# A larger part of an output projection among the steps of a state recurrence

## The chip, the cores and the metric

The kernel runs on one core of one Trainium2 chip. The metric is the device time of one execution in microseconds (us). Before the change three runs gave 1123.08, 1124.1 and 1125.31 us; their median, 1124.1 us, is the time before.

## The reference, cut to what matters

One layer of a hybrid trunk runs over 640 tokens (128 of context, 512 latent ones) of width 1024:

```python
h = rms_norm(x, norm1_g) * (1 + scale1) + shift1
proj = h @ w_in
y_a = rwkv_mixer(shifted proj, s0, ...)   # 8 heads of 64, two directions
y_b = fourier_mixer(...)                  # "FNet", 256 channels
y_c = pool_mixer(...)                     # pooling, 256 channels
mixed = concatenate([y_a, y_b, y_c])      # 1024 channels
x = x + gate1 * (mixed @ w_out)
h = rms_norm(x, norm2_g) * (1 + scale2) + shift2
x = x + gate2 * (relu(h @ w_ff1) ** 2 @ w_ff2)
```

The shift, scale and gate terms, called the modulation here, are `silu(cond) @ w_ada + b_ada`, with one `cond` for the context tokens and one for the latent ones.

## The kernel before, in words

**Tiles.** Channels lie on the 128 partitions and tokens on the free axis, so 1024 channels are 8 blocks (`KB`) of 128 x 640. A product in full precision is made of three fast matmuls: every weight and activation tile is split in a high part (ScalarE copy) and a low part (a subtraction on VectorE or GpSimd), and `gemm_steps` (L333) issues high x high, high x low and low x high for each half of 320 tokens, so 6 matmuls for one 128 x 128 weight block (a "kb" below).

**Order.** `build` (L274) writes the instructions out in one fixed order for each engine. Up to the last state group, `run_groups` (L1367) chooses that order with a clock of its own (`Clock`, L164): fixed and per-element costs of each engine's operations, and for a DMA a fixed part and a rate. The state recurrence (`prep`, `group`) consists of 24 groups: four head pairs j = 0 to 3, three token ranges, two directions. When all six groups of a pair have ended, `post` (L1337) normalises its output y and stores it to the DRAM tile `ycd[j]`.

Beside the groups stand queues of other work. `gemms` holds large products, of which one matmul or two at a time are put where a group would leave TensorE waiting for over 50 ns of that clock (`gemm_step`), or where their share falls under the floor `MR` (0.15, but zero in the second of four stages of six groups); where no product is ready and the gap is over 150 ns, a matmul on a mask (`lmask`, 128 x 512), whose result nobody reads, is issued instead. `side`, `aux` and `slow` hold work that is stepped between the groups.

When the remaining input projection (`in_rest`) has ended, `second` (L1563) puts into `gemms` the modulation for shift2, scale2 and the two gates (`ada_steps`, L390: 64 weight tiles of 256 KB, loaded `AH` = 3 ahead), and into `slow` one task, `more`, that runs `fnet` (L566), then `pool_mix` (L629), then `prepare_out` (L1525), one after the other. `prepare_out` loads `ycd[4]` to `ycd[7]` (FNet and pooling) and splits them to `mh` and `ml`, transposes x into `x1`, and then appends `out_half` (L1508) to `gemms`: the product of the lower four kb of `w_out` for all 8 output blocks b, each added to `x1` under its gate by three VectorE operations (`gated`, L1501). What the queues still hold when the last group has ended is written out behind it, round robin.

**Behind the groups** (L1595 to L1620) the kernel loads `ycd[0]` to `ycd[3]`, splits them, and makes for each block b the upper four kb of `w_out` (24 matmuls), adds them to `x1` with `gated`, splits the scaled result into `h2h` (ScalarE) and `h2l` (VectorE), squares it (ScalarE) and sums the squares (`ssq`, GpSimd). The first block of `w_ff1` follows (8 kb, 48 matmuls, `ahead`), then the statistics of the norm, then the rest of the feed-forward part, in which TensorE sets the pace to the end.

Every operation passes through one wrapper (`Timed`, L251), so the profile shows line L251 for all; the tile names tell them apart: `raw`, `whi`, `wlo` are a weight block and its parts, `wa` modulation weights, `xr`, `W`, `EB`, `bda`, `P`, `X`, `oopa` belong to a state group, `pb` is a PSUM bank (8 in all).

Of the kernel before, what the change touches and what calls it, by code (L numbers as in the profile page):

```python
# [55 lines left out]
AH = 3  # L56
# [46 lines left out]
RS = 1024.0  # L103
AHEAD = 4
# [59 lines left out]
class Clock:  # L164
# [4 lines left out]
    DMA = 2200.0  # L169
    BW = 180.0  # L170
    BWL = 100.0
# [102 lines left out]
def build(nc, tc, T):  # L274
# [115 lines left out]
    def ada_steps(ks, slots, nk, ahead, queue=None):  # L390
# [14 lines left out]
        for n, (k, h, k2) in enumerate(todo):  # L405
# [13 lines left out]
            yield  # L419
# [577 lines left out]
    aux, preps, side, slow, gemms = queues = [[] for _ in range(5)]  # L997
# [14 lines left out]
    tail = [None]  # L1012
# [324 lines left out]
    def post(c):  # L1337
# [27 lines left out]
        S.dma_start(ycd[j][:], y[:])  # L1365

    def run_groups(todo):  # L1367
# [20 lines left out]
        def gemm_step():  # L1388
            t = clock.free["P"]
            step(gemms)  # L1390
            spent[0] += clock.free["P"] - t

        while todo or active or prepared or preps:
# [15 lines left out]
            if then and tail[0].state == "end" and not aux:  # L1409
                then.pop(0)()  # L1410

            urgent = [q for q in (side, aux) if q and not any(x[0] in ctx for x in todo) and todo]
            for n in range(q_.NB):
# [10 lines left out]
                for q in ((aux, slow, side) if slow and turn % q_.SLT == 0 else (aux, side, slow)):  # L1424
# [15 lines left out]
            if gemms and (late_g and used[0] < q_.URG * used[1] or spent[0] < q_.MR * (now - t0)):  # L1440
# [82 lines left out]
    es2 = ExitStack()  # L1523

    def prepare_out():  # L1525

        rx = es2.enter_context(tc.tile_pool(name="rx", bufs=1, side="right"))
        ra = mcs.enter_context(tc.tile_pool(name="ra", bufs=1, side="right"))
        x1 = late["x1"] = rx.tile([P, KB, NT], F32, name="x1")
        mh = late["mh"] = ra.tile([P, 4, NT], F32R, name="mh")  # L1530
        ml = late["ml"] = ra.tile([P, 4, NT], F32R, name="ml")
        loads = [ycd[4 + kb][:] for kb in range(4)] + [x for x in xin]
        place = []

        def load():
            if loads:
                src = loads.pop(0)
                place.append(ra.tile([P, D], F32, tag="xq", name="xq", bufs=2))
                S.dma_start(place[-1][:, 0:src.shape[1]], src)

        load()
        load()
        for kb in range(4):
            yc = place.pop(0)[:, 0:NT]
            yield yc
            S.copy(mh[:, kb, :], yc)
            yield
            (G if EPL else V).tensor_tensor(ml[:, kb, :], yc, mh[:, kb, :].bitcast(F32), op=ALU.subtract)
            yield
            load()  # L1550
        for t in range(5):
            x = place.pop(0)
# [461 lines left out]
```

## Time and profile before

| | before |
|---|---|
| median of 3 runs | 1124.1 us (1123.08 to 1125.31) |
| the profiled execution | 1125.89 us |
| its span, first to last instruction | 1124.1 us |
| TensorE busy | 1075.0 us (96%) |
| VectorE busy | 649.2 us (58%) |
| ScalarE busy | 566.1 us (50%) |
| GpSimd busy | 375.5 us (33%) |
| mean granted TensorE clock | 0.983 of full |

The page lists TensorE as PE (matmuls) and PEld (weight loads, which overlap them), VectorE as DVE, ScalarE as ACT, GpSimd as POOL, and the queue that issues most DMAs as SP. Ends of pipelined matmuls are modelled, so a start-to-start distance tells more of their cost than a duration. Idle time of an engine matters only where something later waits for it.

### The profile page before, as it was taken

What the parts mean: (1) busy time and instruction counts of PE and PEld (TensorE: products, weight loads), DVE (VectorE), ACT (ScalarE), POOL (GpSimd) and SP (SyncE); (2) the same over time, 40 slices, a digit from 0 to 9 for tenths busy, and PEclk for the clock granted to TensorE, in tenths of its full rate; (3) what the DMA queues carried; (4) which work ended last, traced back from release to release, by engine and by line L of the source; (5) the groups of instructions that cost most, each with busy time, mean ns of one, the idle gap of its engine ahead of it and who ended that gap; (6) DMA issues with size and microseconds to landing.
All of it is one profiled execution on the core that took longest, in us unless ns stands there. A gap on an engine that the chain in (4) does not pass through costs nothing.

```text
span 1124.1 us, 23713 instructions
## 1 busy us (share of the span) xinstructions
PE 1075.0 (96%) x9364; PEld 927.2 (82%) x9372; DVE 649.2 (58%) x1462; ACT 566.1 (50%) x1417; POOL 375.5 (33%) x445
## 2 busy tenths in 40 slices
PE   5999999999999998998999899999999999999996
PEld 3688878888786665655688799999999999999996
DVE  5256665457756564757754674773782287139513
ACT  5224576556467454664674265762572176126511
POOL 4224422123322231473500173354343235343120
PEclk9999999999999999999999999999999999999999
DMA  9523311211214345542321321225133123211312
GB/s 316 196 43 92 98 38 43 64 52 47 81 58 140 97 150 143 149 129 86 87 80 43 102 85 57 76 84 160 58 94 94 57 76 104 85 52 53 103 38 94
DMA packets 117712, 104.11 MB, mean 93 GB/s; under 512 B 8925, under 2 KB 95970, under 8 KB 117602
## 3 DMA queue, kind: packets, MB, share of 16 engines
q1 hardware_dynamic: 101618, 81.22, 23.5%
q10 hardware_dynamic: 15552, 21.05, 6.3%
q8 instruction: 74, 1.21, 0.5%
q0 software_dynamic: 432, 0.33, 0.2%
q14 instruction: 36, 0.29, 0.1%
HBM read 90.52 MB, written 9.76 MB: 89 GB/s over the span
## 4 chain that ended last, share of the span: by engine, by line
PE 74%; issue 8%; DVE 8%; ACT 3%; POOL 3%; DMA 2%; ACTq 1%; SPq 0%; POOLq 0%; DVEq 0%
PE pb L251 74%; DMA raw<-w_ff 1%; DVE t L251 1%; ACT pb L251 1%; DVE EB L251 1%; ACTq L251 1%; DVE bda L251 1%; POOL st L251 1%; POOL wlo L251 1%; DMA wa<-w_ada 1%; DVE P L251 1%; DVE BK L251 0%; DMA x<-x_sample 0%; ACT fh L251 0%; DVE op L251 0%
## 5 line engine op out<-in xcount | busy, mean ns | idle before, releaser
L251 POOL TENSOR_TENSOR wlo<-raw,whi 128x512 fp32r<-128x512 f32 x77 | 105.3, 1370 | 144.5 <-ACT whi L251 143.2
L251 PE MATMUL pb<-op,fhi 128*128 128x320 f32 x672 | 147.9, 308 | 0.0
L251 ACT CAST whi<-raw 128x512 fp32r<-128x512 f32 x113 | 70.0, 621 | 146.5 <-PE pb L251 105.1
L251 DVE SCALAR_TENSOR_TENSOR x<-pb,mod,x 128x128 f32<-128x128 f32 (+1 forms) x144 | 55.1, 434 | 147.6 <-PE pb L251 147.5
L251 PE MATMUL pb<-fh,whi 128*128 128x320 f32 (+2 forms) x408 | 123.1, 309 | 1.1 <-ACT fh L251 1.1
L251 PE MATMUL pb<-fl,whi 128*128 128x320 f32 (+2 forms) x408 | 123.1, 309 | 0.2
L251 PEld LDWEIGHTS pb<-op,fhi 128*128 128x128 f32 x672 | 112.4, 188 | 0.0
L251 PE MATMUL pb<-op,flo 128*128 128x320 f32 x336 | 103.5, 308 | 0.0
L251 PE MATMUL pb<-hhi,whi 128*128 128x320 f32 (+1 forms) x304 | 100.1, 334 | 0.0
L251 PE MATMUL pb<-hlo,whi 128*128 128x320 f32 (+1 forms) x304 | 99.5, 332 | 0.0
L251 PE MATMUL pb<-fh,wlo 128*128 128x320 f32 (+2 forms) x408 | 94.9, 308 | 0.3 <-POOL wlo L251 0.3
L251 POOL TENSOR_TENSOR flo<-rw,fhi 128x512 fp32r<-128x512 f32 x36 | 55.3, 1548 | 103.6 <-ACT fhi L251 84.5
L251 POOL TENSOR_TENSOR t<-t,k 128x256 f32<-128x256 f32 (+1 forms) x24 | 16.3, 679 | 205.9 <-DVE t L251 195.2
L251 PE MATMUL pb<-hhi,wlo 128*128 128x320 f32 (+1 forms) x304 | 79.4, 331 | 0.0
L251 PEld LDWEIGHTS pb<-fh,whi 128*128 128x128 f32 x408 | 76.5, 188 | 1.6 <-ACT fh L251 1.6
L251 PEld LDWEIGHTS pb<-fl,whi 128*128 128x128 f32 x408 | 76.6, 188 | 0.7 <-DVE fl L251 0.7
L251 ACT COPY W<-pb 128x256 f32<-128x256 f32 (+3 forms) x144 | 54.5, 399 | 41.2 <-DVE W L251 29.1
L251 PEld LDWEIGHTS <-bda 128*128 128x128 f16 x880 | 43.0, 99 | 37.7 <-issue 14.0
L251 PEld LDWEIGHTS pb<-fh,wlo 128*128 128x128 f32 x408 | 68.7, 188 | 0.5 <-POOL wlo L251 0.5
L251 POOL TENSOR_TENSOR st<-st,halfm 128x1 f32<-128x1 f32 (+2 forms) x19 | 24.2, 1275 | 125.6 <-DVE st L251 125.6
L251 PEld LDWEIGHTS pb<-hlo,whi 128*128 128x128 f32 x304 | 58.8, 194 | 7.6 <-issue 5.1
L251 ACT CAST bda<-pb 64x256 f16<-64x256 f32 (+1 forms) x192 | 63.8, 332 | 1.7
(285 smaller groups left out, 2713.2 us busy)
## 6 DMA issues: line engine op xcount, KB each, us to landing
raw<-w_ff SPq DMA_DIRECT2D x80, 256.0 KB, 2.8
wa<-w_ada SPq DMA_DIRECT2D x64, 256.0 KB, 3.1
rw<-w_ff SPq DMA_DIRECT2D x24, 512.0 KB, 3.6
wa<-w_ada SPq DMA_DIRECT2D x16, 512.0 KB, 8.9
raw<-w_in SPq DMA_DIRECT2D x30, 256.0 KB, 3.0
raw<-w_out SPq DMA_DIRECT2D x16, 256.0 KB, 2.9
ukd<-shq ACTq DMA_DIRECT2D x9, 320.0 KB, 2.5
ds<-dft_s ACTq DMA_DIRECT2D x8, 257.0 KB, 2.7
```

The lines of the kernel that those rows point to most:

```text
L251: return fn(out, *a, **k)
```

## The change

Of the output projection only the kb of the last head pair (j = 3) stays behind the groups. `out_half` becomes `out_part`, which runs twice: over the lower four kb once the modulation has ended, and over the three kb of the pairs 0 to 2 once pair 2 is done. The last pair's y is split from SBUF (`y3`) and no longer goes through DRAM; its weights are loaded and split by `out_last` once the second part has ended. `fnet` and `pool_mix` are two tasks in two queues (`slow`, `slow2`), and `prepare_out` starts when both have ended. From the start of the modulation on, products get at least the share `GR` = 0.3 of the planner's TensorE time while one is ready. Behind the groups the 6 matmuls of the last pair's kb for block b alternate with the first block of `w_ff1` for kb b - 1. The planner's DMA model is faster. The diff, cut:

```diff
-AH = 3
+AH = 5
...
+GR = 0.3
...
-    DMA = 2200.0
+    DMA = 1900.0
     BW = 180.0
-    BWL = 100.0
+    BWL = 260.0
...
             V.tensor_copy(asb[:], ps[:])
-            yield
+            yield asb[:]
...
-    aux, preps, side, slow, gemms = queues = [[] for _ in range(5)]
+    aux, preps, side, slow, slow2, gemms = queues = [[] for _ in range(6)]
...
-    tail = [None]
+    tail = [None, SimpleNamespace(state="end")]
...
-        S.dma_start(ycd[j][:], y[:])
+        if j < NJ - 1:
+            S.dma_start(ycd[j][:], y[:])
+        else:
+            mh, ml = late["y3"]
+            S.copy(mh[:, 0, :], y[:])
+            V.tensor_tensor(ml[:, 0, :], y[:], mh[:, 0, :].bitcast(F32), op=ALU.subtract)
...
-            step(gemms)
+            n = next((n for n, x in enumerate(gemms) if hasattr(x.state, "tensor") and x.state.tensor.name.startswith("asb")), None)
+            if n is None:
+                n = next((n for n, x in enumerate(gemms) if x.ready <= t + 200.0), 0)
+            if not gemms[n].step():
+                gemms.pop(n)
...
-            if then and tail[0].state == "end" and not aux:
+            if then and all(t.state == "end" for t in tail) and not aux:
...
-                for q in ((aux, slow, side) if slow and turn % q_.SLT == 0 else (aux, side, slow)):
+                for q in (aux, side, slow, slow2) if turn % 2 else (aux, side, slow2, slow):
...
+            if "ada" in late and "since" not in late:
+                late["since"] = now, spent[0]
+            since = late.get("since")
+            short = since and spent[0] - since[1] < GR * (now - since[0]) and min([x.ready for x in gemms], default=SLT) <= now + q_.GE
+            if gemms and (late_g and used[0] < q_.URG * used[1] or spent[0] < q_.MR * (now - t0) or short):
...
-            if gap > q_.GAP and gemms and gemms[0].ready <= now + q_.GE:
+            if gap > q_.GAP and gemms and min(x.ready for x in gemms) <= now + q_.GE:
...
-    def out_half():
-
-        w = wsplit(w_out, 0, 1, G if EWO else V)
+    def out_part(r0, nk, m):
+
+        def load(b):
+            if b < KB:
+                r = wp.tile([P, 4, P], F32, tag="raw", name="raw", bufs=RB)
+                dma(r[:, 0:nk], w_out[:, r0:r0 + nk, b * P:(b + 1) * P])
+                hi, lo = [wp.tile([P, 4, P], F32R, tag=n, name=n) for n in ("whi", "wlo")]
+                S.copy(hi[:, 0:nk], r[:, 0:nk])
+                (G if EWO else V).tensor_tensor(lo[:, 0:nk], r[:, 0:nk], hi[:, 0:nk].bitcast(F32), op=ALU.subtract)
+                return hi, lo
+
+        w = load(0)
         for b in range(KB):
             pss = [pm(), pm()]
-            for k4 in range(4):
-                if k4 == 1 and b + 1 < KB:
-                    w2 = wsplit(w_out, (b + 1) * P, 1, G if EWO else V)
-                for _ in gemm_steps(pss, w, (late["mh"], late["ml"]), k4, k4 == 0, k4 == 3):
+            for k4 in range(nk):
+                if k4 == 1:
+                    w2 = load(b + 1)
+                for _ in gemm_steps(pss, w, m, k4, k4 == 0, k4 == nk - 1):
                     yield w[1]
                 yield w[1]
             w = w2
             for h in range(2):
                 gated(late["x1"][:, b, :], pss[h], h, 2, b, late["x1"][:, b, :])
 
...
+    def out_last():
+
+        late["w"] = []
+        for n in range(2):
+            r = wp.tile([P, 4, P], F32, tag="raw", name="raw", bufs=RB)
+            dma(r[:], w_out[:, 3, 512 * n:512 * (n + 1)].rearrange("p (b c) -> p b c", c=P))
+            yield r[:]
+            late["w"].append(wsplit(None, 0, 0, V, r, [wp.tile([P, 4, P], F32R, tag="whi", name="whi"),
+                                                       ra[0].tile([P, NT], F32R, tag="xq", name="w3l", bufs=2)[:, 0:512].rearrange("p (a b) -> p a b", b=P)]))
+            yield
...
-        loads = [ycd[4 + kb][:] for kb in range(4)] + [x for x in xin]
...
+        def take(m, n, loads):
+            for kb in range(n):
+                yc = place.pop(0)[:]
+                yield yc
+                S.copy(m[0][:, kb, :], yc)
+                (G if EPL else V).tensor_tensor(m[1][:, kb, :], yc, m[0][:, kb, :].bitcast(F32), op=ALU.subtract)
+                yield
+                load(loads)
+
+        loads = [ycd[c][:] for c in range(4, 8)] + [x[:, 512 * q:512 * q + 512] for x in xin for q in range(2)]
+        load(loads)
+        load(loads)
+        m = mixed(4)
+        yield from take(m, 4, loads)
...
+        while late["ada"].state != "end":
+            yield 500
+        part = task(out_part(4, 4, m))
+        gemms.insert(0, part)
+        while 2 not in done:
+            yield 500
+        loads = [ycd[c][:] for c in range(3)]
+        load(loads)
+        load(loads)
+        while part.state != "end":
+            yield 500
+        m = mixed(3)
+        yield from take(m, 3, loads)
+        part = task(out_part(0, 3, m))
+        gemms.insert(0, part)
+        while part.state != "end":
+            yield 500
+        yield from out_last()
...
-        gemms.append(task(ada_steps((2, 4, 3, 5), [(wp, "whi", WB), (wp, "wlo", WB)], 1, AH)))
-
-        def more():
-            yield from side_pool("fp", fnet)
-            yield from side_pool("fp2", pool_mix)
-            yield from prepare_out()
-
-        slow.append(task(more()))
+        late["ada"] = task(ada_steps((2, 4, 3, 5), [(wp, "whi", WB), (wp, "wlo", WB)], 1, AH))
+        gemms.append(late["ada"])
+
+        fp = fps.enter_context(tc.tile_pool(name="fp", bufs=1, side="right"))
+        fp2 = fps.enter_context(tc.tile_pool(name="fp2", bufs=1, side="right"))
+        tail[0] = task(fnet(fp))
+        tail[1] = task(pool_mix(fp2))
+        slow.append(tail[0])
+        slow2.append(tail[1])
+
+    fps = ExitStack()
+
+    def third():
+        fps.close()
+        slow.append(task(prepare_out()))
...
-    then.append(second)
+    then.extend([second, third])
...
-        mh = mo.tile([P, 4, NT], F32R, name="mh2")
-        ml = mo.tile([P, 4, NT], F32R, name="ml2")
-        for kb in range(4):
-            yc = mo.tile([P, NT], F32, tag="yc", name="yc2", bufs=4)
-            dma(yc[:], ycd[kb][:])
-            S.copy(mh[:, kb, :], yc[:])
-            V.tensor_tensor(ml[:, kb, :], yc[:], mh[:, kb, :].bitcast(F32), op=ALU.subtract)
         ssq = mo.tile([P, NT], F32, name="ssq")
-        for b in range(KB):
-            pss = gemm(w_out, b * P, (mh, ml), G, (0,))
-            xb = x1[:, b, :]
-            for h in range(2):
-                gated(xb, pss[h], h, 2, b, xb)
-            for i, cs in SEG:
-                S.activation(h2h[:, b, cs], xb[:, cs], AF.Copy, scale=gs2[:, b, i:i + 1])
-                V.scalar_tensor_tensor(h2l[:, b, cs], xb[:, cs], gs2[:, b, i:i + 1], h2h[:, b, cs].bitcast(F32), op0=ALU.mult, op1=ALU.subtract)
-            if b == 0:
-                S.activation(ssq[:], xb, AF.Square)
-            else:
-                sq = mo.tile([P, NT], F32, tag="sq", name="sq", bufs=2)
-                S.activation(sq[:], xb, AF.Square)
-                G.tensor_tensor(ssq[:], ssq[:], sq[:], op=ALU.add)
-        ahead = [gemm(w_ff1, 0, (h2h, h2l), G, extra=2)]
+        wf = [wsplit(w_ff1, 0, 0, G)]
+        pf = [pm(), pm()]
+        for b in range(KB + 1):
+            if b < KB:
+                pss = [pm(), pm()]
+                whi, wlo = [x[:, b % 4:b % 4 + 1, :] for x in late["w"][b // 4]]
+                gemm_kb(pss, (whi, wlo), late["y3"], 0, True, True)
+                xb = x1[:, b, :]
+                for h in range(2):
+                    gated(xb, pss[h], h, 2, b, xb)
+                for i, cs in SEG:
+                    S.activation(h2h[:, b, cs], xb[:, cs], AF.Copy, scale=gs2[:, b, i:i + 1])
+                    V.scalar_tensor_tensor(h2l[:, b, cs], xb[:, cs], gs2[:, b, i:i + 1], h2h[:, b, cs].bitcast(F32), op0=ALU.mult, op1=ALU.subtract)
+                if b == 0:
+                    S.activation(ssq[:], xb, AF.Square)
+                else:
+                    sq = mo.tile([P, NT], F32, tag="sq", name="sq", bufs=2)
+                    S.activation(sq[:], xb, AF.Square)
+                    G.tensor_tensor(ssq[:], ssq[:], sq[:], op=ALU.add)
+            if b == 4:
+                wf.append(wsplit(w_ff1, 0, 1, G))
+            if b:
+                gemm_kb(pf, wf[(b - 1) // 4], (h2h, h2l), b - 1, b == 1, b == KB, 2)
+        es4.close()
+        ahead = [pf]
...
-    nc = bacc.Bacc("TRN2", target_bir_lowering=False, num_devices=1, dynamic_dma_scratch_size=4096)
+    nc = bacc.Bacc("TRN2", target_bir_lowering=False, num_devices=1, dynamic_dma_scratch_size=1024)
```

## Rows read from the trace of the kernel before

**Rows 1.** The page, part 4: the chain that ended last, shares of the span by engine.
```profile
PE 74%; issue 8%; DVE 8%; ACT 3%; POOL 3%; DMA 2%; ACTq 1%; SPq 0%; POOLq 0%; DVEq 0%
```

**Rows 2.** Windows: stretch, length, PE, PEld, DVE, ACT, POOL busy (instructions), clock, DMA.
```profile
345.00:592.00 247.00, 231.25 (x2617) 155.05 (x2619) 154.68 (x404) 144.39 (x409) 87.04 (x127) 0.97 0.39 118
592.00:620.00 28.00, 27.47 (x279) 23.49 (x279) 14.05 (x36) 11.58 (x29) 0.00 (x0) 0.94 0.17 49
620.00:634.20 14.20, 10.28 (x50) 7.79 (x51) 7.10 (x16) 1.25 (x2) 1.99 (x1) 0.88 0.06 18
634.20:679.80 45.60, 45.60 (x313) 45.60 (x312) 32.16 (x59) 25.01 (x44) 28.39 (x20) 1.00 0.37 112
775.00:800.00 25.00, 25.00 (x173) 25.00 (x172) 10.91 (x20) 5.54 (x11) 7.39 (x6) 1.00 0.17 53
```

**Rows 3.** Windows of the mask matmuls alone on PE: stretch, length, busy (matmuls), clock, DMA.
```profile
345.00:592.00 247.00, 15.43 (x47) 0.97 0.39 118
```

**Rows 4.** Windows of tile wa alone (the modulation): PE, PEld, clock, DMA.
```profile
345.00:550.00 205.00, 38.65 (x128) 5.34 (x128) 0.97 0.42 126
```

**Rows 5.** Windows of tile ml alone: PE, PEld, DVE, POOL, clock, DMA.
```profile
592.00:634.20 42.20, 13.92 (x41) 8.22 (x41) 0.00 (x0) 0.00 (x0) 0.92 0.13 38
```

**Rows 6.** PE in order of time: the first block of w_ff1 begins, the norm's sums begin.
```profile
672.68 0.31 PE L251 MATMUL pb<-h2h,whi 128*128 128x320 f32 x1
...
679.80 1.17 PE L251 MATMUL pb<-ones,ssq 128*128 128x1 f32 x10
```

**Rows 7.** DVE in order of time: the last y, then blocks behind the groups.
```profile
633.30 0.89 DVE L251 TENSOR_TENSOR y<-pb,y 128x512 f32<-128x512 f32 x2
...
652.25 1.12 DVE L251 SCALAR_TENSOR_TENSOR x<-pb,mod,x 128x128 f32<-128x128 f32 x3
653.30 0.42 DVE L251 SCALAR_TENSOR_TENSOR h2l<-x,gs,h2h 128x128 fp32r<-128x128 f32 x1
654.17 0.75 DVE L251 SCALAR_TENSOR_TENSOR h2l<-x,gs,h2h 128x512 fp32r<-128x512 f32 x1 [0.45 <-ACT h2h L251]
655.14 1.13 DVE L251 SCALAR_TENSOR_TENSOR x<-pb,mod,x 128x128 f32<-128x128 f32 x3 [0.21 <-PE pb L251]
...
659.71 2.08 DVE L251 SCALAR_TENSOR_TENSOR h2l<-x,gs,h2h 128x128 fp32r<-128x128 f32 x2
```

**Rows 8.** Tile mh: splits of the last four ycd tiles (min/median/max ns, first to last start).
```profile
L251 ACT CAST mh<-yc x4: 728/730/731, 640.7 to 643.8; 128x640 fp32r<-128x640 f32 x4
L251 DVE TENSOR_TENSOR ml<-yc,mh x4: 814/818/826, 641.4 to 644.7; 128x640 fp32r<-128x640 f32 x4
```

**Rows 9.** POOL in order of time, beside the blocks of rows 7.
```profile
654.84 1.58 POOL L251 TENSOR_TENSOR ssq<-ssq,sq 128x640 f32<-128x640 f32 x1 [1.26 <-ACT sq L251]
...
659.67 1.30 POOL L251 TENSOR_TENSOR wlo<-raw,whi 128x512 fp32r<-128x512 f32 x1
```

**Rows 10.** PE in order of time: two products behind a group step.
```profile
602.35 0.41 PE L251 MATMUL pb<-ml,whi 128*128 128x320 f32 x1
602.60 0.31 PE L251 MATMUL pb<-mh,whi 128*128 128x320 f32 x1
```

**Rows 11.** Tiles ycd and xq from 525 us on: ns, first to last start.
```profile
L251 ACTq DMA_DIRECT2D xq<-ycd x4: 326/358/444, 528.6 to 544.8; - x4
L251 ACTq DMA_DIRECT2D ycd<-y x1: 326/326/326, 541.5 to 541.5; - x1
...
L251 PE MATMUL pb<-ident,xq x40: 272/273/329, 560.7 to 584.4; 128*128 128x128 f32 x40
```

**Rows 12.** DMA issues: count, KB each, median us to landing.
```profile
raw<-w_out SPq DMA_DIRECT2D x16, 256.0 KB, 2.9
```

**Rows 13.** Windows: columns as in rows 2.
```profile
525.00:550.00 25.00, 22.62 (x203) 14.82 (x201) 17.48 (x41) 11.49 (x34) 10.00 (x14) 0.80 0.30 94
```

**Rows 14.** PE in order of time: products early in the kernel, at the lower clock.
```profile
77.42 0.47 PE L251 MATMUL pb<-hlo,whi 128*128 128x320 f32 x1
77.69 0.47 PE L251 MATMUL pb<-hhi,whi 128*128 128x322 f32 x1
```

More of the change, by code (lines that the diff above doesn't have):

```diff
@@ L1439, in run_groups @@
                 used = [0.0, 0.0]
-            if gemms and (late_g and used[0] < q_.URG * used[1] or spent[0] < q_.MR * (now - t0)):
+            if "ada" in late and "since" not in late:
[3 more added lines that the diff above has]
+            if gemms and (late_g and used[0] < q_.URG * used[1] or spent[0] < q_.MR * (now - t0) or short):
                 t = clock.free["P"]
@@ L1525, in prepare_out, with mixed @@
+    ra = []
+    def mixed(n):
+        return [ra[0].tile([P, 4, NT], F32R, tag="m" + x, name="m" + x)[:, 0:n, :] for x in "hl"]
     def prepare_out():
         rx = es2.enter_context(tc.tile_pool(name="rx", bufs=1, side="right"))
-        ra = mcs.enter_context(tc.tile_pool(name="ra", bufs=1, side="right"))
+        ra.append(es3.enter_context(tc.tile_pool(name="ra", bufs=1, side="right")))
         x1 = late["x1"] = rx.tile([P, KB, NT], F32, name="x1")
-        mh = late["mh"] = ra.tile([P, 4, NT], F32R, name="mh")
@@ L1531, in prepare_out, with load @@
-        ml = late["ml"] = ra.tile([P, 4, NT], F32R, name="ml")
-        loads = [ycd[4 + kb][:] for kb in range(4)] + [x for x in xin]
+        late["y3"] = [ra[0].tile([P, 1, NT], F32R, name=f"y3{x}") for x in "hl"]
         place = []
-        def load():
+        def load(loads):
             if loads:
                 src = loads.pop(0)
-                place.append(ra.tile([P, D], F32, tag="xq", name="xq", bufs=2))
+                place.append(ra[0].tile([P, NT], F32, tag="xq", name="xq", bufs=2))
@@ L1539, in load @@
                 S.dma_start(place[-1][:, 0:src.shape[1]], src)
-        load()
-        load()
-        for kb in range(4):
[L1544 to L1550, printed above, removed]
+        def take(m, n, loads):
[6 more added lines that the diff above has]
+                load(loads)
@@ L1551, in prepare_out @@
+        loads = [ycd[c][:] for c in range(4, 8)] + [x[:, 512 * q:512 * q + 512] for x in xin for q in range(2)]
[3 more added lines that the diff above has]
+        yield from take(m, 4, loads)
         for t in range(5):
-            x = place.pop(0)
-            yield x[:]
             for q in range(2):
+                x = place.pop(0)
+                yield x[:]
                 ps = pm()
                 for i in range(4):
-                    PE.transpose(ps[:, i * P:(i + 1) * P], x[:, (4 * q + i) * P:(4 * q + i + 1) * P], ident[:])
+                    PE.transpose(ps[:, i * P:(i + 1) * P], x[:, i * P:(i + 1) * P], ident[:])
@@ L1558, in prepare_out @@
                 yield
                 S.copy(x1[:, 4 * q:4 * q + 4, t * P:(t + 1) * P], ps[:].rearrange("p (a b) -> p a b", a=4))
-            load()
-        gemms.append(task(out_half()))
+                load(loads)
[7 more added lines that the diff above has]
+        load(loads)
+        load(loads)
@@ L1585, in build @@
     QW = 4 * HB
+    es4 = es3
     es3 = ExitStack()
```

3 lines of the change are left out of this document (1 added, 2 removed).

## The prediction

> **What bounds the kernel now.** The chain of waits comes first: TensorE holds 74% of it, "issue" and VectorE 8% each [rows 1]. So a microsecond is won only where TensorE idles, does work that nobody reads, or is made to wait less. The windows then cut the stretch that the change touches, from the start of the modulation (345 us) to the first sums of the second norm (679.8 us) [rows 2]. Three parts stand there. From 345 to 592 TensorE is busy 231.25 of 247 us, idle 15.75. From 592 to 620 the last groups run with the first `out_half` products between them, and from 620 to 634.2 the last pair's post-processing, busy 10.28 of 14.2. From 634.2 to 679.8 it is busy all of the 45.6 us and waits for nothing. Of the 231 busy us, 15.43 are 47 mask matmuls, which only fill gaps [rows 3]. So 15.4 + 15.75 = 31.2 us of the long stretch is room, and 45.6 us behind it is work that could use room. The question is how much of that work goes into the room, and how much displaces group steps.
>
> **The share for the modulation.** It has 38.65 us of TensorE in 205 us, 19% [rows 4]. A floor of 0.3 binds: it would end some 129 us after its start (38.65/0.3), near 474 instead of 550. That moves products earlier and adds none, so by itself I cost it at nothing; its use is that `out_part` can begin.
>
> **Behind the last y.** Of `out_half`'s 64 low-part matmuls (`ml`), 41 are done by 634.2 [rows 5]; 23 are left, so 3 x 23 = 69 matmuls in all. The dense rate, in the stretch from 775 us, is 25.00/173 = 0.1445 us [rows 2]. So the 45.6 us are 69 matmuls (10.0), 192 of the upper kb (27.7) and the block of `w_ff1` from 672.68 to 679.80 (7.1) [rows 6], 44.8 in sum. After the change 48 products of the last pair remain, with those of `w_ff1` between them: 12 for a block, 1.73 us, less than VectorE needs. VectorE's period for a block, where TensorE hardly held it up, was 655.14 - 652.25 = 2.89 us: three gated additions, then 0.42, a wait of 0.45 for ScalarE, and 0.75 [rows 7]. I take 2.89 for each of 8 blocks, 23.1 us. In front stand the copy and the subtraction that split y (0.73 + 0.82) [rows 8] with 0.2 for hand-overs, and six matmuls (0.88) with 0.2; behind, the last six of `w_ff1` (0.88) with 0.2 and about 0.6 for the last sum of squares. That is 27.6 us for 45.6: **18.0 us gained**. The bounds: VectorE's own operations without a wait, 1.05 + 0.42 + 0.75 = 2.2 for a block, give 22 us, a gain of 23.5; and 1.05 + 2.08 = 3.13, where the two subtractions took 2.08 together [rows 7], give 29.5, a gain of 16.
>
> What made them 2.08 stands on GpSimd: a `wlo` subtraction began at 659.67, 0.04 us before them, and ended at 660.97; in the 2.89 us block GpSimd's sum of squares, 1.58 us, began after both [rows 9]. The Trainium skill's page "SBUF — State Buffer", section "SBUF: two separate sides", says that a VectorE operation with two SBUF inputs and a GpSimd operation that reads SBUF exclude each other for whole instructions. The two rows agree. By that rule the squares, which stay, could make every block 3.13 us, and the sum below would be 1.9 us worse. I keep 2.89, since the per-block `wlo` that collided goes away and only two remain.
>
> The round trip of the last y through DRAM and four loads go as well. Today the 69 matmuls cover them (TensorE never idles there), so they are worth nothing beyond this.
>
> **What goes in among the groups.** The 69 matmuls and the three kb of pairs 0 to 2 (3 x 8 x 6 = 144): 213 x 0.1445 = **30.8 us**. A product alone behind a group step costs more: 602.60 - 602.35 = 0.25 us before the next could start, 0.105 over the dense rate [rows 10]. If bursts are of four, 53 bursts x 0.105 = **5.6 us**; the ends are nothing (all join bursts that exist) and 22.4 (each alone).
>
> **What room takes back.** With a product ready most of the time I let all mask matmuls go, **15.4 us** (ends 0 and 15.4), and half of the 15.75 us of idle, **7.9** (ends 0 and 15.75). Half, because part of that idle is real waiting for another engine, which products in front only shorten.
>
> **Edits costed at nothing.** More VectorE work falls among the groups: 48 gated additions for the 13 there now, and eight more weight splits, some 17 us; it is busy 154.7 of 247 there [rows 2], so this is covered, unless a gated addition waits for its product with a group's operation queued behind it. Each such wait is bounded by one burst, 0.6 us, and by zero. ScalarE issues five more loads of x in halves and three of `ycd`, and starts FNet's and pooling's loads together; its 144.4 of 247 us hide them. SP loses four loads and gains eight smaller ones. GpSimd takes three more splits of 1.5 us at 35% load. The planner's DMA figures change the order before 345 us too; with nothing to price it by, zero, ends -2 and +2.
>
> **Sum:** -18.0 + 30.8 + 5.6 - 15.4 - 7.9 = -4.9 us, against the profiled execution's own 1125.9: 1121.0. The median of the runs lies 1.8 under it, so the forecast is **1119.2 us**.
>
> **Rivals.**
>
> *The floor displaces group steps.* The share of 0.3 inserts a product even where a group step is ready. What is then late next is the group chain, whose xr and W products each depend on the one before. Place: 474 to 592 us. For it: TensorE is already busy 94% there, and the idle is spread in small waits for other engines. Against it: 592 to 620 took products into a chain-bound stretch and kept TensorE busy 27.47 of 28. Price: masks go, but no idle comes back and bursts are half as long (11.2): -18.0 + 30.8 + 11.2 - 15.4 = +8.6, 1132.7 us. It decides once less than 30.8 + 5.6 - 18.0 = 18.4 us of room is recovered. Chance 0.20.
>
> *The second part starts too late.* It needs pair 2's post (541.5 us), the end of part one, and three loads with splits; today the four loads and the transposes of `prepare_out` stretch from 528.6 to 584.4 [rows 11]. If a third of it, 48 products (6.9 us), falls behind the groups, 3.9 us of post idle take some, and `out_last` then stands open: a load of 2.9 us [rows 12] and splits. Some 5 us worse, 1124 us: no change. A share that failed to bind would end here too. Chance 0.17.
>
> *All idle comes back.* Products in front of waiting steps cover the waits whole: another 7.9 us, 1111.3. For it, the products are ready in small steps; against it, the waits that remain at 620 to 634. Chance 0.12.
>
> *The clock drops behind the last y.* TensorE is active 1.73 of 2.89 us there, in bursts. From 525 to 550, with 2.4 us idle, the granted clock was 0.80 [rows 13], while in 592 to 620 it was 0.94. At 1.2 GHz two products start 0.27 us apart [rows 14], so a block takes 12 x 0.27 = 3.2 us on TensorE instead of VectorE's 2.89: 2.5 us worse, 1121.7. The Trainium skill's page "TensorE: Matmul & The Clock Gate", section "Why this matters for your kernels", advises against idle gaps between bursts for this reason; the windows agree that the clock fell near idle, though not that gaps this short do it. Chance 0.06.
>
> **How the numbers follow.** About 0.2% (2.2 us) is what a measurement here can tell from no change; the three runs spread as much. The forecast has 0.45, its own range 1112 to 1123 from the bounds of idle, bursts and block period. Faster: most of 0.45, the 0.12, and little of the other cases, 0.60. Same: the late second part and the clock case for the most part, 0.17. Slower: displacement and an edge, 0.23. The range 1108 to 1130 reaches into both sides and leaves about 2 in 10 out.
>
> **What would show it.** Right: from about 474 us products of `mh`, few mask matmuls after 345 us, TensorE idle under 8 us up to the last groups; the last `y` at about 647 us, the sums of the norm 28 us later, with VectorE the busiest engine between. Wrong: the groups' end over 18 us later than 620 us, so that the tail's gain is spent; products of part two behind the last y; or a block period over 3.2 us.

## The result, and the profile after

Four runs of the changed kernel gave a median of 1175.91 us (1172.86 to 1179.19), four of the kernel before 1123.59: a ratio of 1.0466, 95% interval 1.0429 to 1.0503. The change is slower by 52 us, where 5 less were forecast, and the time lies far outside the range. The profiled execution took 1177.77 us, its span is 1176.0.

The first view is the chain of the kernel after (page, part 4), beside [rows 1].

```profile
PE 73%; DVE 7%; issue 7%; DMA 5%; ACT 4%; POOL 3%; ACTq 0%; SPq 0%; POOLq 0%; DVEq 0%
```

TensorE still holds it; the DMA share grew from 2% to 5%. The windows tell more (columns as in [rows 2], the cuts at the events that cut those: the last `y` goes to its normalisation at 677, is split at 690.4, and the sums of the second norm begin at 725.4; a fourth stretch follows the sums).

```profile
345.00:677.00 332.00, 309.52 (x3076) 211.76 (x3075) 185.69 (x473) 164.90 (x455) 92.86 (x130) 0.94 0.33 100
677.00:690.40 13.40, 9.92 (x45) 7.26 (x44) 7.62 (x16) 1.14 (x3) 1.98 (x1) 0.75 0.11 33
690.40:725.40 35.00, 26.18 (x139) 22.59 (x138) 28.09 (x54) 18.33 (x34) 18.49 (x12) 0.87 0.18 53
725.40:740.00 14.60, 14.60 (x77) 14.60 (x78) 2.45 (x8) 2.82 (x8) 5.04 (x4) 0.72 0.12 36
```

Up to the end of the last groups it is 332 us, where before it was some 276 (345 to 621): 56 us lost, where the sum had priced 13 (30.8 + 5.6 - 15.4 - 7.9). Behind the last y 45.6 became 35.0: 10.6 gained, where 18.0 were priced. The last row is a loss outside that cut: 77 matmuls took 14.6 us at a clock of 0.72. Before, 75 took 10.2 there:

```profile
679.80:690.00 10.20, 10.20 (x75) 10.19 (x74) 1.85 (x5) 2.73 (x6) 4.98 (x4) 1.00 0.26 75
```

Two further rows of the kernel after are windows of one tile each on TensorE (length, busy time with the count, clock, DMA): the modulation (tile `wa`, with its weight loads as a second busy time), then the mask matmuls.

```profile
345.00:526.00 181.00, 53.40 (x128) 7.01 (x128) 0.95 0.51 155
...
300.00:680.00 380.00, 12.08 (x41) 0.95 0.32 96
```

The modulation grew from 38.65 us [rows 4] to 53.40 with the same 128 instructions. Its last matmul began at 518.7 us, where the prediction had its end near 474. The masks, which were all to vanish, went from 54 (17.54 us in the same cut before) to 41. TensorE in order of time shows why the modulation grew:

```profile
350.78 1.06 PE L252 MATMUL pb<-wa,sil 128*32 128x512 f32 x6
351.77 1.09 PE L252 MATMUL pb<-W 64*64 64x128 f32 x16
352.79 1.04 PE L252 MATMUL pb<-wa,sil 128*32 128x512 f32 x2
353.77 0.35 PE L252 MATMUL pb<-X,bda 128*128 128x64 f16 x6
```

Six of these instructions (three weight tiles) hold TensorE for 351.77 - 350.78 = 0.99 us, two (one tile) for 0.98. In the kernel before, eight (four tiles) held it for 451.32 - 450.32 = 1.00:

```profile
450.32 1.06 PE L251 MATMUL pb<-wa,sil 128*32 128x512 f32 x8
451.32 0.29 PE L251 MATMUL pb<-P,bda 128*128 128x64 f16 x4
```

Each tile's product uses a strip of 32 columns at its own `tile_position`, and by these rows products on different strips run beside each other. The floor asks for a product as soon as one is ready, so more tiles go out singly, 36 of the 64 where it was 19, and each of those costs what three or four cost in one go. The Trainium skill's page "TensorE: Matmul & The Clock Gate", section "Why this matters for your kernels", says that outputs of few rows, put on distinct column groups, run concurrently; these rows agree.

How far the state groups came is read from one of their matmuls, `W,xr` (320 in the whole kernel), counted by stretch: first the kernel before, then the one after, each time from 345 to 425 us and from 425 to 500:

```profile
L251 PE MATMUL pb<-W,xr 128*64 128x64 f32 x56 | 4.2, 225 | 0.0
...
L251 PE MATMUL pb<-W,xr 128*64 128x64 f32 x52 | 3.8, 224 | 0.0
```

```profile
L252 PE MATMUL pb<-W,xr 128*64 128x64 f32 x44 | 3.5, 236 | 0.0
...
L252 PE MATMUL pb<-W,xr 128*64 128x64 f32 x20 | 1.6, 224 | 0.0
```

108 steps became 64. ScalarE in order of time shows where some were lost (ACTq is its queue of DMA issues; in these rows no arithmetic of ScalarE starts until the issues in front of it are out):

```profile
352.54 1.00 ACTq L252 DMA_DIRECT2D px<-fpd  x1
353.57 1.72 ACTq L252 DMA_DIRECT2D rc<-rcnt  x2
359.85 0.33 ACTq L252 DMA_DIRECT2D px<-fpd  x1
361.24 1.79 ACTq L252 DMA_DIRECT2D rc<-rcnt  x2
363.07 0.37 ACT L252 COPY y<-pb 128x256 f32<-128x256 f32 x1 [10.79 <-DMA px<-fpd]
...
433.76 0.33 ACTq L252 DMA_DIRECT2D ycd<-y  x1
434.20 0.37 ACTq L252 DMA_DIRECT2D ds<-dft_s  x1
434.62 0.52 ACTq L252 DMA_DIRECT2D k<-ukd  x1
...
436.99 1.04 ACTq L252 DMA_DIRECT2D s<-state  x2
441.68 0.33 ACTq L252 DMA_DIRECT2D ds<-dft_s  x1
442.06 0.31 ACT L252 ACTIVATE xr<-pb,pc 64x64 f32<-64x64 f32 x1 [16.23 <-DMA s<-state]
```

For 10.8 us pooling's loads kept ScalarE from any step of a group, and for 16.2 us the store of pair 1 (`ycd<-y`), FNet's matrices (`ds`) and the loads of pair 3 did.

### The profile page after: what moved, and what is told of

Read it like the earlier page. It is cut to its first block, busy times and chain, and to the rows that moved or that the text cites. A ratio compares the mean times of both kernels' runs of the same rounds, so it can differ in the third digit from the quotient of the medians.

```text
span 1176.0 us, 23683 instructions
## 1 busy us (share of the span) xinstructions
PE 1109.7 (94%) x9338; PEld 939.6 (80%) x9338; DVE 659.0 (56%) x1493; ACT 564.5 (48%) x1419; POOL 370.7 (32%) x440
## 4 chain that ended last, share of the span: by engine, by line
PE 73%; DVE 7%; issue 7%; DMA 5%; ACT 4%; POOL 3%; ACTq 0%; SPq 0%; POOLq 0%; DVEq 0%
PE pb L252 73%; DMA wa<-w_ada 2%; DMA raw<-w_ff 2%; DVE t L252 1%; ACT pb L252 1%; POOL wlo L252 1%; DVE h2l L252 1%; DVE x L252 1%; DVE EB L252 1%; DVE bda L252 1%; DVE P L252 1%; DMA xq<-x_sample 0%; ACTq L252 0%; ACT fh L252 0%; DMA x<-x_sample 0%
## 5 line engine op out<-in xcount | busy, mean ns | idle before, releaser
L252 DVE SCALAR_TENSOR_TENSOR x<-pb,mod,x 128x128 f32<-128x128 f32 (+1 forms) x168 | 64.6, 433 | 155.9 <-PE pb L252 155.9
L252 POOL TENSOR_TENSOR wlo<-raw,whi 128x512 fp32r<-128x512 f32 x69 | 93.0, 1351 | 148.1 <-ACT whi L252 148.1
L252 ACT CAST whi<-raw 128x512 fp32r<-128x512 f32 (+1 forms) x115 | 70.2, 612 | 135.9 <-PE pb L252 103.5
L252 POOL TENSOR_TENSOR t<-t,k 128x256 f32<-128x256 f32 (+1 forms) x24 | 16.7, 695 | 190.0 <-DVE t L252 176.4
L252 PE MATMUL pb<-wa,sil 128*32 128x512 f32 x192 | 68.7, 639 | 4.8 <-DMA wa<-w_ada 4.8
L252 ACT ACTIVATE xr<-pb,pc 64x64 f32<-64x64 f32 x72 | 22.3, 309 | 89.0 <-DVE xr L252 70.9
```

The costliest lines, as they stand in the source:

```text
L252: return fn(out, *a, **k)
```

## The experiments

Each row is one kernel: the start of the last pair's normalisation on TensorE (the end of the groups) and the start of the norm's sums, both from the profiled execution, and the time, with the difference to the kernel before in the same session (all in us). The time is a median where runs are more than one; a single run carries no interval of its own.

| kernel | groups end | sums begin | time (runs) | to before |
|---|---|---|---|---|
| before | 621.5 | 679.8 | 1123.6 (4) | |
| after | 677.2 | 725.3 | 1175.9 (4) | +52.3 |
| e1 after, no floor | 645.7 | 722.8 | 1174.6 (1) | +53.9 |
| e2 after, old DMA figures | 680.2 | 722.3 | 1171.3 (1) | +50.7 |
| e3 after, modulation by two | 667.3 | 709.1 | 1159.2 (1) | +38.6 |
| e4 after, pooling behind FNet | 713.7 | 754.8 | 1204.8 (1) | +84.1 |
| e5 after, no products | 664.7 | 705.6 | 1153.4 (1) | +29.2 |
| e6 before, floor 0.3 | 677.1 | 733.0 | 1179.7 (1) | +55.6 |
| e7 before, FNet beside pooling | 637.4 | 697.0 | 1142.6 (1) | +18.5 |
| e8 before, modulation by four | 628.4 | 686.7 | 1132.4 (4) | +8.3 |
| e9 before, planner nudged 2% down | 637.1 | 695.4 | 1141.9 (1) | +18.1 |
| e10 before, new DMA figures | 626.9 | 686.1 | 1133.0 (1) | +9.2 |
| e11 before, floor 0.2 | 636.0 | 695.9 | 1142.0 (1) | +18.2 |
| e12 before, modulation by two | 630.0 | 688.3 | 1134.1 (1) | +10.3 |
| e13 after, loads on SP | 658.9 | 707.2 | 1159.2 (4) | +34.4 |
| e14 before, loads on SP | 618.7 | 677.3 | 1123.6 (10) | -1.2 |
| e15 before, planner nudged 2% up | 625.3 | 687.0 | 1133.3 (1) | +8.5 |
| e16 after, planner nudged | 661.2 | 708.7 | 1157.7 (1) | +32.9 |
| e17 after, loads on SP, by two | 670.4 | 710.7 | 1157.7 (4) | +37.1 |
| e18 as e17, floor 0.2 | 625.3 | 701.5 | 1148.0 (4) | +27.5 |

**One part undone (e1 to e4).**

```diff
e1: -GR = 0.3            +GR = 0.0
e2: -DMA = 1900.0, BWL = 260.0, AH = 5   +2200.0, 100.0, 3
e3: +            if both and k2 % 2 == 0:
    +                continue              (two tiles, then their matmuls; six loads ahead)
e4: -        slow2.append(tail[1])    +        slow.append(tail[1])
```

> The changed kernel with the fixed share set to zero; everything else stays. Theory A (the floor of 0.3 displaces group steps: modulation weights go out one by one, about 1 us of TensorE each, ahead of steps that are ready) expects most of the 52 us back: about 1135 us, the modulation at 40 us of TensorE instead of 53, pair 2 stored near 555 us instead of 595. Theory B (the planner's faster DMA figures let TensorE stand behind loads that have not landed) expects it still slow, about 1165 us. Theory C (FNet and pooling side by side crowd the groups) expects about 1165 us too.

> The changed kernel with the planner's DMA figures of before (2200 ns and 100, three loads ahead instead of 1900 and 260, five ahead). Theory B expects the waits of TensorE for modulation and FNet loads to go (some 10 us) and with them up to half of the loss: 1145 to 1160 us. Theory A expects 1165 us or more: the share stays binding. Theory C: 1170 us.

> The changed kernel, but the modulation issues two weight tiles at a time (two column strips of the array run at once), six loads ahead. If single matmuls on a 32-column strip are what makes the modulation dear (theory A, first half), its TensorE time falls from 53 to some 35 us and the kernel to about 1155 us. If the cost of the share is only that it comes first, whatever it issues, the modulation's time falls too but the kernel stays at 1165 us or more.

> The changed kernel with pooling behind FNet in one queue, as before; everything else stays. Theory C expects the crowding of 350 to 450 us to go and the kernel at about 1155 us. Theories A and B expect 1170 to 1185 us: the groups are displaced as now, and prepare_out starts later, so more of part two falls behind the last y.

Without the floor (e1) the two signs of theory A came, a modulation of 41.00 us and pair 2 stored at 553.4, and the groups end 31 us earlier; but its time did not: the products then drain behind the groups, and the sums begin only 2.5 us earlier. So the floor delays the groups, yet taking it out of the change gives nothing back. The DMA figures (e2) changed the time by 4.6 us, not by the 16 to 31 of theory B. Tiles by two (e3) cut the modulation to 31.53 us and the time by 17. Pooling behind FNet (e4) is 29 us worse than the kernel after, past all its theories: the preparation comes later, and up to 760 us 116 masks stand where products would (41 after).

**One part alone, or left out (e5 to e8).**

```diff
e5: -        part = task(out_part(4, 4, m))     +        part = task(iter(()))     (both parts)
e6: before, + the lines of `since` and `short`, GR = 0.3
e7: before, + `slow2`, `tail[1]` and `third`
e8: before, +            if four and k2 % 4 < 3:
            +                continue           (four tiles, then their matmuls)
```

> The changed kernel with both runs of out_part left out: 336 products (192 of the lower four kb, 144 of pairs 0 to 2), their weights' loads and splits and their 48 gated additions go, so the output lacks seven of the eight kb of the projection. Everything else (the share, the modulation, FNet beside pooling, the new tail) stays. At the dense rate of 0.1445 us the products are 48.6 us. Theory A, the products displace the groups one for one and no more: about 1176 - 49 = 1127 us. Theory B, each product also costs switching, a lower clock and waits for its gated additions: under 1115 us. Theory C, most products sat in room that would otherwise hold masks and idle: over 1145 us, with some 60 more mask matmuls.

> The kernel before with one rule added: the floor of 0.3 for products from the start of the modulation on. Nothing else changes, so out_half stays at four kb and the old tail stays. The floor brings the modulation forward one tile at a time. Theory A, a modulation matmul on one strip of 32 columns costs about 0.98 us of TensorE whether or not its three neighbours run beside it, and the floor breaks up the groups of two and more: modulation 50 us or more instead of 38.65, and 1130 to 1140 us. Theory B, the floor only moves products: 1117 to 1124 us, modulation still near 39 us. Theory C, the floor displaces group steps and idle comes on top: over 1145 us.

> The kernel before with FNet and pooling as two tasks in two queues, and the preparation of the projection behind both; no share, no parts, old tail, old DMA figures. In the changed kernel putting pooling back behind FNet cost 29 us. Theory A, side by side they start the projection's preparation earlier, more of out_half's 192 products fall among the groups and the tail shrinks by up to 23 x 0.29 us: 1112 to 1119 us. Theory B, the gain belongs to the changed kernel only, where two parts wait for the preparation: 1119 to 1124 us. Theory C, both tasks press on the groups of pairs 1 and 2 and delay them: over 1128 us, pair 2 stored later than 550 us.

> The kernel before with one thing changed: the modulation waits for four weight tiles (six loads ahead instead of three) and issues their four matmuls, one on each strip of 32 columns, in one go. Four such matmuls back to back took 1.05 us in the trace, one alone 0.98 to 1.04. So 64 tiles need 16 x 1.05 = 17 us of TensorE instead of 38.65, 21.8 us less. Theory A, TensorE's time among the groups is the bound, so the projection's products and groups move up: 1100 to 1110 us. Theory B, the freed time turns into mask matmuls and idle because the modulation only filled gaps: 1117 to 1124 us, with masks up by 15 us or more. Theory C, waiting for four loads holds products back and the groups lose their filler: over 1124 us.

e5 fits its theory C, at 1153: leaving out 336 products of 48.6 us took only 22.6 us off the time, and masks came in their place. From 527 us on there are 122 masks, where the kernel after has 13 (3.65 us):

```profile
527.00:680.00 153.00, 34.73 (x122) 0.92 0.08 22
```

So in this late stretch there was room for products, some 31 us. What makes the kernel 29 us slower even without any of them lies mostly before it: at 527 us e5 had made 192 `W,xr` steps, the kernel before 240. e6 shows one cause: the floor alone, on the kernel before, loses 56 us. Its `W,xr` steps in the same two stretches, and its windows of the modulation and of the masks:

```profile
L252 PE MATMUL pb<-W,xr 128*64 128x64 f32 x40 | 3.0, 227 | 0.0
...
L252 PE MATMUL pb<-W,xr 128*64 128x64 f32 x24 | 1.7, 222 | 0.0
```

```profile
300.00:600.00 300.00, 52.56 (x128) 0.95 0.35 108
...
300.00:680.00 380.00, 46.57 (x161) 0.96 0.30 92
```

64 steps for 108, as in the kernel after, a modulation of 52.56 us, and 161 masks (54 before): the filler is spent early in place of group steps, and when the groups, each step of which waits for the one before, leave gaps afterwards, nothing is left to put in. Time taken from such a chain wasn't given back by the room that came later.

This doesn't hang on one order. By 500 us the nine kernels of the table with the floor at 0.3 had made 176 to 192 `W,xr` steps, the eleven with a lower floor or none 200 to 224; and in the table the groups of the nine end between 658.9 and 713.7 us, those of the eleven between 618.7 and 645.7.

e7 loses 18.5 us, e8 8.3 (1.0077, 1.0049 to 1.0106), although its modulation takes only 21.69 us of TensorE. Both times fall under their theory C, but two unlike edits with like losses raise the question whether the edit is the cause; hence the next four.

**The order by itself (e9 to e12).**

```diff
e9:  -    DMA = 2200.0     +    DMA = 2150.0
e10: the kernel before with DMA, BWL and AH of the change
e11: e6 with GR = 0.2
e12: the edit of e3 on the kernel before
```

> The kernel before with one figure of the planner's clock changed by 2%: the fixed part of a DMA 2150 instead of 2200. No work is added or removed; only the order the planner writes out can differ. Theory A, the order is robust and differences of 8 to 55 us in the runs so far each have a cause in what was edited: 1121 to 1127 us. Theory B, the groups' order is so finely set that any perturbation of the planner costs: 1132 to 1145 us, so that of a loss of 18 us (FNet beside pooling alone) or 8 us (modulation by four tiles) nothing can be put down to the edit itself.

> The kernel before with the planner's new DMA figures alone (fixed part 1900, load rate 260, modulation loads five ahead). The new figures promise loads earlier than the trace shows them. In the changed kernel the old figures were worth 4.6 us. Theory A, they are worth about as much here: 1126 to 1131 us. Theory B, they do nothing without the other parts: 1121 to 1126 us. Theory C, a disturbed order costs as much as any part of the change: over 1135 us.

> The kernel before with the floor at 0.2 instead of the 0.3 of the run that took 1180 us. The modulation's natural share is 38.65 of 205 us, 0.19, so this floor hardly binds. Theory A, what costs is the size of the share, by group steps displaced that are not won back: 1122 to 1135 us, and 50 or more of the W,xr matmuls between 345 and 425 us (56 before, 40 with 0.3). Theory B, what costs is that a floor is there at all (it breaks up the modulation's groups and puts single tiles ahead of ready steps): over 1150 us.

> The kernel before with the modulation two tiles at a time, six loads ahead. Modulation on TensorE 31.5 to 33 us instead of 38.65, and it ends no later than 540 us. Theory A, the 6 us come off the groups: 1115 to 1120 us. Theory B, they turn into mask matmuls, since it was filler: 1121 to 1126 us, with 15 or more masks more. Theory C, as by four tiles, the filler becomes coarser, TensorE stands idle between, and it is slower: 1127 to 1135 us.

e9 and e12 came out as their last theories had it, e10 and e11 between theirs (e11 with 48 `W,xr` steps up to 425 us, where its theory A asked for 50). A figure of the planner moved by 2%, with no work added, costs 18 us. With e15 (+8.5 the other way) that makes two draws of another order, and e7, e8, e10, e11 and e12 (+8 to +19) are of the same size. So no such loss can be put down to its edit; what can is e6 (+56), and by the same measure the change as a whole. At 0.2 the floor, beside a natural share of 0.19, costs no more than a nudge: on the kernel before it is its size that costs.

**The same order, other queues; and a second draw (e13 to e16).** In e13 and e14 the planner writes the same order for the four engines; SP issues the loads of FNet, pooling and the pairs.

```diff
+    Q = Timed(clock, "S", nc.sync)
-            S.dma_start(c[n][:], ukd[j][i][:])
+            Q.dma_start(c[n][:], ukd[j][i][:])
...
e15: before, DMA = 2250.0          e16: after, DMA = 1850.0
```

> The changed kernel, its order on TensorE, VectorE, ScalarE and GpSimd kept to the last instruction; only the loads of FNet (transform matrices, weights, its two channels), of pooling (weights, counts, its two channels) and of each head pair (k, r, v, two states) are issued by SP instead of ScalarE. In the changed kernel's trace ScalarE stood still for such loads 10.8 us at 352 to 363 and 16.2 us at 426 to 442, in which no step of the state chain was made. Theory A, these stops are what FNet beside pooling costs: 20 to 27 us back, 1149 to 1157 us. Theory B, the chain waits for the landed data anyhow, or other engines set the pace: 1170 to 1178 us. Theory C, the loads now stand behind modulation weights in SP's order and land later: over 1180 us.

> The kernel before with the same edit: order kept on four engines, the loads of FNet, pooling and the pairs issued by SP. Before, ScalarE stood still 8.8 us once for pooling's loads. Theory A: that stop comes back, 1112 to 1120 us. Theory B: it was hidden, 1121 to 1127 us. Theory C: SP's order delays the loads, over 1127 us.

> The kernel before, the fixed part of a DMA in the planner 2250 instead of 2200, the other way from the run with 2150 (1142 us). Theory A, any other order than the one that stands costs 8 to 20 us, since nothing in the planner's own time tells good orders from bad: 1131 to 1144 us. Theory B, 2150 hit one unlucky spot: 1121 to 1127 us.

> The changed kernel with the fixed part of a DMA in the planner 1850 instead of 1900: the same structure in another order. Theory A, the order is a draw of some 10 to 20 us on top of a structure that costs by itself: 1165 to 1190 us. Theory B, the changed kernel's loss is an unlucky draw: under 1150 us.

e13 took 1159.2 us (1.0319, 1.0280 to 1.0358, against the kernel before): 16.7 us back, short of the 20 to 27 of theory A, but nearer to it than to B or C. On its ScalarE the stop for pooling's loads is gone, and the one at 426 is shortened to this one. In it the store of pair 1 still stands, issued at 425.27; the last 2.9 us are a wait for VectorE:

```profile
428.19 0.31 ACT L252 ACTIVATE xr<-pb,pc 64x64 f32<-64x64 f32 x1 [10.84 <-DVE xr L252]
```

10.8 + (16.2 - 10.8) = 16.2 us of stops are gone, and 16.7 us of time. That the two agree so well is in part luck. The order of the engines is the same, so the profiled executions (spans 1176.0 and 1155.6) can be laid side by side: e13 is 2.9 us ahead before the first stop (the `X` of ScalarE at 350.55 and 347.61), 8.6 behind it (`y` on VectorE, 380.05 and 371.47), 8.5 before the second (`dd`, 437.48 and 428.98), 15.6 behind it (`asb`, 461.67 and 446.10) and 20.4 at the end. So 12.7 us are won at the two stops, and the rest elsewhere. In the kernel before the same edit does nothing (1.0001, 0.9982 to 1.0019), though ScalarE stood still for pooling's loads there too (8.8 us). That stop was hidden: without it ScalarE waits for TensorE instead (first the kernel before, then e14):

```profile
445.48 1.19 ACT L251 COPY oopa<-pb 64x512 f32<-64x512 f32 x2 [8.84 <-DMA px<-fpd]
...
448.47 0.65 ACT L251 COPY W<-pb 128x256 f32<-128x256 f32 x2 [6.92 <-PE pb L251]
```

e16, between its theories, says that the order of the kernel after was an unlucky one: a nudge took 18 us off it, without any other edit, but 33 stayed. That bounds what e3's 17 us, made with a free order, prove of the modulation.

**Both (e17, e18).**

> The changed kernel with both edits that each took about 17 us off it: loads of FNet, pooling and pairs issued by SP (1159 us), and the modulation two tiles at a time (1159 us). Theory A, they are two causes, ScalarE's stops and TensorE time in lone modulation matmuls, and add: 1139 to 1147 us. Theory B, each mostly gave the planner's order another draw, and they overlap: 1152 to 1162 us.

> As the run before this one, with the floor for products at 0.2 instead of 0.3. The modulation needs some 32 us of TensorE, so at 0.2 it ends near 505 us instead of 500 or earlier, and more group steps come first. Theory A, what is left of the loss is group steps displaced by the floor and not won back: at least 8 us less than the run before. Theory B, the floor buys in the tail what it costs among the groups, as leaving it out altogether showed: within 5 us of it.

They didn't add, as theory B had it: e17 took 1157.7 us (1.0308, 1.0241 to 1.0374), about what e13 and e3 took alone, and its four runs spread from 1145.4 at a mean clock of 0.974 to 1161.1 at 0.960. e18 is 9.7 us below it (1.0226, 1.0174 to 1.0278); the intervals overlap, so that difference isn't settled. What its trace tells is plain (windows of the last groups, then of what follows up to the sums):

```profile
548.40:625.30 76.90, 74.59 (x927) 62.93 (x928) 45.56 (x122) 41.95 (x110) 6.53 (x11) 0.93 0.16 46
625.30:701.50 76.20, 58.69 (x311) 52.46 (x309) 47.16 (x95) 25.36 (x46) 24.81 (x16) 0.82 0.17 51
```

Its groups end at 625.3, within 4 us of the kernel before, and 76.2 us follow up to the sums where the kernel before has 58.3: the products of pairs 0 to 2 all stand behind the groups, and TensorE idles 17.5 us in that tail. e17, with more of them among the groups, has 45 us more in front and 36 less behind. No profile of the changed structure has the sums before 701 us, against 679.8.

## Why the prediction was wrong

**"That moves products earlier and adds none, so by itself I cost it at nothing."** This is the step that failed most. The floor of 0.3 broke the modulation into single tiles, +14.75 us of TensorE, and put products before steps of the chain: alone it cost 55.6 us (e6), and with it the groups ended at 658.9 us or later in every kernel tried. Inside the change that is only half of the matter, since without the floor (e1) the products fell behind the groups and the time stayed. The forecast had counted on both at once, groups on time and products among them; no run shows both. The rival "the floor displaces group steps" had the mechanism, but began it at 474 us. It shows earlier: with the floor alone (e6) 24 steps stand from 425 to 500 us where there were 52. Its price, an 8.6 us loss, assumed that the masks would go; they fell only from 54 to 41, and with the floor alone they rose to 161. It also named the decision point: under 18.4 us of room recovered. Masks gave 5.5, and TensorE's idle time, from the store of pair 0 (298.8 and 295.4 us) to the sums, grew from 381.0 - 359.2 = 21.8 to 429.9 - 392.7 = 37.2 (columns as in [rows 2]; first before, then after):

```profile
298.80:679.80 381.00, 359.16 (x3815) 269.15 (x3821) 238.32 (x586) 211.83 (x565) 130.31 (x167) 0.97 0.35 104
```

```profile
295.40:725.30 429.90, 392.65 (x3827) 280.45 (x3827) 251.32 (x619) 213.85 (x572) 126.63 (x162) 0.94 0.31 93
```

**"... its 144.4 of 247 us hide them"**, of ScalarE's loads. ScalarE was far from full, but what counted is how long an issue waits with arithmetic behind it. With the order held, moving the loads away took 16.7 us off (e13 against after), some 13 of them at the two stops. I counted its busy time and not who is queued behind the wait.

**"With a product ready most of the time I let all mask matmuls go".** The room behind 527 us is real (e5), but it comes after the loss. TensorE's busy time in the two rows above rose by 33.5 us: 14.75 are the modulation, -5.5 the masks. Of the rest, some 24, about 4 are 24 matmuls of the input projection that the later cut takes in, and by an estimate from the two clocks, 359.16 x (0.97/0.94 - 1), some 11 are the lower clock; how the remainder divides isn't settled.

**"... with nothing to price it by, zero, ends -2 and +2"**, of an order that changes. Two nudges priced it, at 8.5 and 18.1 us. The order of the kernel before is better than each of its seven neighbours tried (e7 to e12 and e15), and the change gave it up with its first edit of the planner. The whole forecast of -4.9 was smaller than this.

**The tail.** Its mechanism held. From the last groups to the sums the kernel before takes 58.3 us, e2 to e4, where hardly a product was left over, 41.1 to 42.1: 16.2 to 17.2 gained for 18.0. In the kernel after that stretch is 48.1: part two ran to 697 us, and the last weights were split late.

```profile
696.53 0.45 PE L252 MATMUL pb<-mh,wlo 128*128 128x320 f32 x2
...
698.66 0.85 PE L252 MATMUL pb<-y3h,w3l 128*128 128x320 f32 x4 [0.95 <-DVE w3l L252]
```

That is the rival "the second part starts too late": 48.1 for 41.1 to 42.1, so 6 to 7 us for its "Some 5". The block's period was (723.88 - 699.13)/8 = 3.09 us, from the first gated addition to the end of the last `h2l`, within the bounds and at the upper one, 3.13. Two rows beside each other (VectorE, then GpSimd):

```profile
717.37 1.76 DVE L252 SCALAR_TENSOR_TENSOR h2l<-x,gs,h2h 128x512 fp32r<-128x512 f32 x1
...
714.95 3.63 POOL L252 TENSOR_TENSOR ssq<-ssq,sq 128x640 f32<-128x640 f32 x2
```

The subtraction, 0.75 us alone [rows 7], ends 0.55 us after GpSimd's squares do. So the squares did collide, and the reason given for 2.89, that only two `wlo` splits remain, was wrong as well: GpSimd made four between these blocks (702.35, 710.36, 713.65 and 718.53 us). 3.13 would have been the better choice. The Trainium skill's page "SBUF — State Buffer", section "SBUF: two separate sides", gives this rule; the rows agree with it, and I should have let it decide.

**The clock behind the last y** was a rival of 0.06. In the blocks it read 0.87 on the mean; its larger part came behind the sums, which I hadn't looked at: 77 x (10.2/75) = 10.5 us of dense work took 14.6, so 4 us. Finer windows of TensorE show what went before (length, busy time, clock, DMA):

```profile
715.00:721.00 6.00, 2.63 (x12) 0.91 0.15 44
721.00:733.80 12.80, 12.28 (x46) 0.51 0.14 42
733.80:740.00 6.20, 6.20 (x45) 1.00 0.15 42
```

TensorE was busy for 2.63 of 6 us, waiting mostly for VectorE's `h2l`; then the clock stood at its lower level, 1.2 GHz, up to about 734. The Trainium skill's page "TensorE: Matmul & The Clock Gate", section "Why this matters for your kernels", warns of gaps between bursts; the fall to 0.51 behind this stretch agrees.

**What is open.** Against the kernel before, the changed kernel and seven variants of it (e4 and e5 apart) lie 27 to 54 us up, the seven neighbours of the kernel before 8 to 19. So some 10 to 45 us belong to the structure. Shown of it are ScalarE's stops, in one order (some 13 of 16.7 us), and the floor's delay of the groups, over all orders; in the total, the floor's price is shown on the kernel before alone (e6). How the rest divides among lone modulation matmuls, products left behind the groups, the clock and the draw of the order isn't settled. The smaller `dynamic_dma_scratch_size` stood in every variant of the change; no run tried it by itself. No kernel of this study beat the one before; e14 equals it.

## What to carry to other kernels

In a kernel whose order a planner writes greedily, nudge the planner first and measure: the spread of that is a price that any edit may pay that touches it, and a forecast below it can't be told from the draw. A floor that runs filler ahead of ready steps of a dependent chain delays the chain, and later room only helps if filler is left for it. When loads are issued by an engine that also computes, count how long each issue may wait and what stands behind it, not how busy the engine is; in the changed kernel the queue of an engine that computes nothing was the better place, in the kernel before it made no difference.

## What was not expected of the hardware

A modulation matmul on 32 columns held TensorE for 0.98 us alone, three together for 0.99, and four for 1.00. Over a whole run the mean granted clock goes with the spread between runs of one kernel: the four of e17 have spans of 1158.5, 1158.8, 1143.6 and 1151.8 us at mean clocks of 0.960, 0.960, 0.974 and 0.967.
